# A hybrid decoder trunk on one core: filter sums on ScalarE and GpSimd, and memory preparation in split passes

## The chip, the cores and the metric

The kernel runs on one core of a Trainium2 chip. TensorE (PE in the profile) multiplies matrices; its weight loads are listed as PEld. VectorE (DVE), ScalarE (ACT) and GpSimd (POOL) do the elementwise work; SyncE (SP) issues the DMAs. The metric is the time of one execution on the device, in microseconds. Lower is better.

## The reference, cut to what matters

Two layers over 1024 tokens of width 1024, everything in float32. The change lies in the first layer's convolution and in what runs beside it.

```python
def conformer_conv(h, w_pw1, b_pw1, w_dw, b_dw, ln_g, ln_b, w_pw2, b_pw2):
    u = h @ w_pw1 + b_pw1
    a, gate = jnp.split(u, 2, axis=-1)
    u = a * jax.nn.sigmoid(gate)
    u = lax.conv_general_dilated(u, w_dw[:, None, :], window_strides=(1,),
        padding=[(CONV_WIDTH - 1, 0)], feature_group_count=D_MODEL, ...) + b_dw   # 31 taps per channel
    u = jax.nn.silu(layernorm(u, ln_g, ln_b))
    return u @ w_pw2 + b_pw2

def memory_cross_attention(h, mem_n, w_q, w_k, w_v, w_o):    # mem_n: 256 tokens, 4 heads
    s = q k^T / sqrt(256), with q = h @ w_q, k = mem_n @ w_k;  p = softmax(s)
    return (p @ (mem_n @ w_v)) @ w_o
...
x = x + conformer_conv(rmsnorm(x), ...)      # layer 0 (layer 1: attention instead)
x = x + memory_cross_attention(rmsnorm(x), rmsnorm(mem), ...)
x = x + (relu(h @ w1) ** 2) @ w2
```

## The kernel before, in words

Activations lie with the 1024 features in eight chunks of 128 partitions and the tokens along the free axis, in two halves of 512 (`HALVES`). A product that must keep float32 precision is made in split passes: an operand is split into a high part, which is a copy rounded to float32r (`act.copy`), and a low part, the difference (`low`, line 148, on VectorE). `passes` (line 262) turns a pair of split operands into three matrix instructions: low times high, high times low, high times high. An operand given as a single tile is multiplied as plain float32, in one `pe.matmul` call.

`conv_layer` (line 293) is the first layer's convolution. For each chunk `m` of channels, `gated_unit` (line 362) makes the two pointwise products on TensorE, a sigmoid on ScalarE and the gated product `u` on VectorE (line 370). `u` is kept with even and odd tokens apart, behind 15 zero columns each. `convolve` (line 386) then applies the 31 taps on VectorE. It uses a shared sum: `both` (lines 396 to 402) is a filter over the odd tokens with the sums of neighbouring taps, 16 instructions; the even outputs add 16 taps over the difference `d0`, and the odd outputs 15 taps over `d1` (line 408). The results go to `X`, and a running sum `acc` (line 354) feeds the layer norm. `layer_norm` (line 306) follows, half by half, and `linear` with `pw2` and `add_x` (line 324) ends the layer.

Beside this runs `memory_matrices` (line 433), once per layer of the whole model: per head it multiplies the memory by `wk` and `wv` (line 458), and these by `wq` and `wo` (lines 479 and 493), and stores the two combined matrices `mqk` and `mvo` in DRAM for `mem_attention`. It is a generator: each `yield` ends one step, 16 steps per layer and 32 in all. `conv_layer` takes one step at a time with `next(prep)`: two ahead of loading X, two in the normalization, two for each chunk, and the rest after the layer norm. These products are all of plain float32. Their weights come through `get` (line 438), 512 KB at a time into three buffers `praw`.

The order on each engine is made at compile time by a list scheduler: among the instructions that are ready by its own estimate, the one that was written first goes first, and `high_priority` moves one ahead. On the chip each engine works through its own list in that order and waits by semaphores. So a preparation step fills TensorE wherever gates and pw2 are not ready. Tiles named `t` in the pool `nrm` share four buffers, used by the normalizations, the squares and, with the change, the terms of the shared sum. GpSimd works in this stage only for small powers (line 207) and the zero columns (line 301).

The first MLP (lines 600 and on), which the prediction uses for comparison, has differences of 128x512 on VectorE (line 148) beside additions of 128x512 on GpSimd (lines 647, 865, 951), and additions from PSUM into SBUF on VectorE (line 967).

Of the kernel before, what the change touches and what calls it, by code (L numbers as in the profile page):

```python
# [12 lines left out]
F32 = mybir.dt.float32  # L13
# [73 lines left out]
def trunk(ctx, tc, a, out):  # L87
# [98 lines left out]
    def add_squares(acc, ch):  # L186

        sq = nrm.tile([P, HALF], F32, name="sq", tag="t", bufs=4)
# [104 lines left out]
    def conv_layer(pm, prep):  # L293
        with tc.tile_pool(name="conv", bufs=2) as cp:
# [3 lines left out]
            def padded():  # L298

                u = cp.tile([P, 2, (PAD + S) // 2], F32, name="u")  # L300
                pool.memset(u[:, :, : PAD // 2], 0.0)
                return u
# [27 lines left out]

            hs = operands()
            ahead = gate_weights(0)
            u = padded()
            for sl in HALVES:
                normalize(hs, "mix0", sl)
                next(prep)
                gated_unit(pm, cp, 0, ahead, hs, u[:, :, PAD // 2 :], sl)
            acc = [cp.tile([P, HALF], F32, name=f"acc{s}", bufs=1) for s in range(2)]
            for m in range(NCH):
                if m:  # L340
                    u = padded()
# [44 lines left out]
    def convolve(cp, m, u, sums):  # L386


        n, k = S // 2, TAPS // 2
        even, odd = u[:, 0, :], u[:, 1, :]  # L390
        d0 = cp.tile([P, n + k], F32, name="d0")
        d1 = cp.tile([P, n + k - 1], F32, name="d1")
        dve.tensor_tensor(d0, even[:, : n + k], odd[:, : n + k], op=ALU.subtract)
        dve.tensor_tensor(d1, even[:, 1 : n + k], odd[:, : n + k - 1], op=ALU.subtract)
        both = cp.tile([P, n], F32, name="both")
        dve.tensor_scalar(
            both, odd[:, :n], sums[:, 0:1], col("dw_b", m), op0=ALU.mult, op1=ALU.add
        )
        for j in range(1, k + 1):
            dve.scalar_tensor_tensor(  # L400
                both, odd[:, j : j + n], sums[:, j : j + 1], both, op0=ALU.mult, op1=ALU.add
            )
        out = [X[:, m, sl] for sl in HALVES]
        for s, d, taps in ((0, d0, k + 1), (1, d1, k)):
            y = both
            for j in range(taps):
                w = col("dw_w", m * TAPS + 2 * j + s)
                dve.scalar_tensor_tensor(  # L408
                    out[s], d[:, j : j + n], w, y, op0=ALU.mult, op1=ALU.add
                )  # L410
                y = out[s]
# [21 lines left out]
    def memory_matrices(pp, pq, layer):  # L433
# [4 lines left out]
        def get(src):  # L438
            raw = pp.tile([P, NCH, P], F32, name="praw", bufs=3)
# [1006 lines left out]
```

## Time and profile before

| | |
|---|---|
| time, median of 3 runs | 2823.84 us (2814.29 to 2826.63) |
| the profiled execution | 2825.31 us, of which the span is 2823.3 us |
| granted TensorE clock, mean | 0.991 |
| busy: PE, DVE, ACT, POOL | 2740.8, 2030.9, 1278.3, 703.1 us |
| first gated chunk complete | 76.7 us |
| first filter tap, last filter tap | 92.0, 387.7 us |
| pw2 ends | 527 us |

How to read it: the span runs from the first to the last instruction of the program in one profiled execution. A group row gives line, engine, operation, output and inputs with their shapes, count, busy time in us, mean length of one in ns, and the idle time of the engine just before, with what ended it. The length of one is longer than the pace at which such instructions follow one another, since the next starts before the last one has written everything. Ends of matrix instructions are modelled.

### The profile page before, as it was taken

Reading aid. Unit: us, or ns where it says so; the run is one execution under the profiler, and the core shown is the slowest. Engines: PE = TensorE matmul, PEld = TensorE weight load, DVE = VectorE, ACT = ScalarE, POOL = GpSimd, SP = SyncE. Lnnn points to the kernel's source line nnn. Section 1 sums busy time; section 2 is a strip of 40 time slices with the busy share of each in tenths; the row PEclk is TensorE's granted clock in tenths of the full one; section 3 lists DMA queues with packets and bytes.
Section 4 is the critical chain, followed back from the end, with each engine's and each line's share of the span. In section 5 each row is a group of like instructions: output and inputs, shape, how many; then the busy total and the mean of one; then the engine's idle time right before and its main releaser. Section 6 shows DMA issues by size and latency. Waiting matters only on the chain.

```text
span 2823.3 us, 36214 instructions
## 1 busy us (share of the span) xinstructions
PE 2740.8 (97%) x12968; PEld 2261.3 (80%) x12968; DVE 2030.9 (72%) x3358; ACT 1278.3 (45%) x2293; POOL 703.1 (25%) x473
## 2 busy tenths in 40 slices
PE   8999999999999999999899999989999999989998
PEld 6777777888888877888688888878888788878886
DVE  5999984555776576777788888875546855577776
ACT  5212143433555553333466666673423655543332
POOL 0000000000065625774000000000000365525773
PEclk9999999999999999999899999999999999999999
DMA  6334364322165585652222221243213455655651
GB/s 219 120 119 135 114 206 124 101 90 70 65 230 177 178 309 187 227 199 89 69 68 70 57 65 55 69 136 98 94 64 105 149 176 190 218 208 197 227 201 61
DMA packets 165428, 390.68 MB, mean 138 GB/s; under 512 B 17264, under 2 KB 46192, under 8 KB 164992
## 3 DMA queue, kind: packets, MB, share of 16 engines
q1 hardware_dynamic: 165248, 388.37, 40.9%
q8 instruction: 102, 1.67, 0.2%
q14 instruction: 78, 0.64, 0.1%
HBM read 270.79 MB, written 113.31 MB: 136 GB/s over the span
## 4 chain that ended last, share of the span: by engine, by line
PE 74%; DVE 12%; ACT 5%; DMA 5%; issue 3%; POOL 1%; SPq 0%; DVEq 0%; POOLq 0%; ACTq 0%
PE mm L1070 34%; PE mm L269 29%; PE mm L1255 5%; DVE w L148 2%; DVE op L148 2%; DVE x L408 1%; PE mm L1341 1%; DVE x L1310 1%; DMA ua<-x 1%; ACT x L1315 1%; PE mm L1353 1%; PE mm L1354 1%; DVE both L400 1%; DVE wl L148 1%; ACT pth L151 1%
## 5 line engine op out<-in xcount | busy, mean ns | idle before, releaser
L1070 PE MATMUL mm<-op,w 128*128 128x512 f32 x5424 | 1242.4, 391 | 24.5 <-ACT m L955 8.7
L1070 PEld LDWEIGHTS mm<-op,w 128*128 128x128 f32 x5424 | 1020.5, 189 | 243.2 <-ACT m L955 9.6
L269 PE MATMUL mm<-op,wh 128*128 128x512 f32 x1056 | 330.5, 394 | 4.2 <-DVE op L148 4.2
L148 DVE TENSOR_TENSOR w<-r,w 128x512 fp32r<-128x512 f32 x264 | 262.6, 998 | 30.5 <-ACT w L653 30.5
L653 ACT CAST w<-r 128x512 fp32r<-128x512 f32 x264 | 163.3, 622 | 262.0 <-PE mm L1070 233.2
L269 PEld LDWEIGHTS mm<-op,wh 128*128 128x128 f32 x1056 | 200.2, 190 | 48.5 <-DVE op L148 6.5
L1255 PE MATMUL mm<-op,wh 128*128 128x512 f32 x736 | 231.4, 396 | 0.0
L148 DVE TENSOR_TENSOR w<-t,w 128x512 fp32r<-128x512 f32 x180 | 178.2, 1005 | 63.2 <-ACT w L653 63.1
L269 PE MATMUL mm<-op,wl 128*128 128x512 f32 x528 | 210.5, 400 | 7.1 <-DVE wl L148 6.2
L207 POOL TENSOR_TENSOR r<-v,mhalf 128x4 f32<-128x4 f32 (+1 forms) x15 | 16.8, 1117 | 741.0 <-DVE v L205 741.0
L647 POOL TENSOR_TENSOR t<-r,t 128x512 f32<-128x512 f32 x104 | 174.9, 1681 | 91.4 <-DVE w L148 54.2
L653 ACT CAST w<-t 128x512 fp32r<-128x512 f32 x180 | 112.0, 622 | 169.8 <-PE mm L1070 140.6
L151 ACT CAST wh<-raw 128x1024 fp32r<-128x1024 f32 x96 | 100.7, 1050 | 193.8 <-PE mm L269 97.5
L865 POOL TENSOR_TENSOR x<-x,x 128x512 f32<-128x512 f32 x112 | 160.2, 1455 | 112.6 <-ACT x L878 101.6
L967 DVE TENSOR_TENSOR x<-mm,x 128x512 f32<-128x512 f32 x160 | 109.5, 684 | 91.1 <-PE mm L1070 73.7
L1255 PEld LDWEIGHTS mm<-op,wh 128*128 128x128 f32 x736 | 139.2, 189 | 26.7
L269 PE MATMUL mm<-op,xsh 128*128 128x512 f32 x512 | 158.0, 393 | 0.0
L1255 PE MATMUL mm<-op,wl 128*128 128x512 f32 x368 | 155.0, 421 | 1.9 <-ACT q L1275 1.9
L151 ACT CAST pth<-mm 128x512 fp32r<-128x512 f32 (+1 forms) x224 | 105.9, 495 | 108.5 <-PE mm L556 80.8
L408 DVE SCALAR_TENSOR_TENSOR x<-d,par,x 128x512 f32<-128x512 f32 x232 | 154.5, 746 | 0.0
L647 POOL TENSOR_TENSOR t<-r,r 128x512 f32<-128x512 f32 x52 | 80.2, 1542 | 295.1 <-DMA r<-in_ff_w 191.0
L1315 ACT ACTIVATE x<-x,nb 128x128 f32<-128x128 f32 (+7 forms) x128 | 99.5, 778 | 109.3 <-DVE nb L1313 100.0
(188 smaller groups left out, 4689.6 us busy)
## 6 DMA issues: line engine op xcount, KB each, us to landing
r<-in_ff_w SPq DMA_DIRECT2D x128, 512.0 KB, 4.0
op<-ua SPq DMA_DIRECT2D x80, 512.0 KB, 6.8
us<-x SPq DMA_DIRECT2D x128, 256.0 KB, 2.9
op<-us SPq DMA_DIRECT2D x64, 512.0 KB, 5.6
raw<-mvo SPq DMA_DIRECT2D x32, 512.0 KB, 3.4
ua<-ul SPq DMA_DIRECT2D x64, 256.0 KB, 2.2
ua<-uh SPq DMA_DIRECT2D x60, 256.0 KB, 2.3
raw<-in_pw SPq DMA_DIRECT2D x24, 512.0 KB, 4.7
```

The costliest lines, as they stand in the source:

```text
L148: dve.tensor_tensor(lo, src, hi.bitcast(F32), op=ALU.subtract)
L151: act.copy(hi, src)
L269: pe.matmul(out_ps, x, y, start=i == 0, stop=i == len(terms) - 1)
L400: dve.scalar_tensor_tensor(both, odd[:, j : j + n], sums[:, j : j + 1], both, op0=ALU.mult, op1=ALU.add)
L408: dve.scalar_tensor_tensor(out[s], d[:, j : j + n], w, y, op0=ALU.mult, op1=ALU.add)
L647: (dve if g in (2, 3, UP, UP + 1) else pool).tensor_tensor(t, raws[g, x], raws[g, y], op=ALU.subtract)
L653: act.copy(highs[n][0], raws[steps[n][:2]])
L865: eng.tensor_tensor(u[g, x], y1, y2, op=op_)
L967: dve.tensor_tensor(v, sums[key], v, op=ALU.add)
L1070: pe.matmul(sums[key], y, z, start=first and i == 0, stop=n == last_of[key] and i == len(terms) - 1, skip_group_check=True,)
L1255: pe.matmul(t, x, y, start=n == 0, stop=n == len(terms) - 1)
L1315: act.activation(x[:, :n], x[:, :n], AF.Exp, bias=nb, accum_out=rs)
```

## The change

The shared sum moves out of `convolve` into `shared_sum`: each of the 16 terms is a multiplication on ScalarE, and 15 additions on GpSimd gather them in `both`. It is written one chunk ahead of the filters, and the gates two chunks ahead, with three fixed tiles `planes` for `u`. In `convolve` the taps add up in one PSUM bank, `acc = bank(pc)`, which both the even and the odd chain use; only the last tap of each writes to `X`. The preparation's pool has three PSUM banks instead of four.

`memory_matrices` splits its operands. The memory is loaded in four pieces and split by ScalarE (high, with the gain) and VectorE (low). `get` loads each weight in two halves; ScalarE makes the high part and GpSimd the low part. The products of keys and values are split as they are read from PSUM. All its products are now made in three passes. Of its 32 steps, two more than before are taken ahead of the layer norm.

```diff
-            for m in range(NCH):
-                if m:
-                    u = padded()
-                    for sl in HALVES:
-                        gated_unit(pm, cp, m, ahead, hs, u[:, :, PAD // 2 :], sl)
-                if m + 1 < NCH:
-                    ahead = gate_weights(m + 1)
+            shared = shared_sum(cp, 0, planes[0], pairs[:, 0])
+            for m in range(-1, NCH):
+                if m + 2 < NCH:
+                    ahead = gate_weights(m + 2)
                 for _ in range(2):
                     next(prep, None)
-                convolve(cp, m, u, pairs[:, m])
+                if m + 2 < NCH:
+                    for sl in HALVES:
+                        gate(m + 2, ahead, sl)
+                if m < 0:
+                    continue
+                now = shared
+                if m + 1 < NCH:
+                    shared = shared_sum(cp, m + 1, planes[(m + 1) % 3], pairs[:, m + 1])
+                convolve(cp, pc, m, planes[m % 3], now)
...
+    def shared_sum(cp, m, u, sums):
+        n, k = S // 2, TAPS // 2
+        odd = u[:, 1, :]
+        both = cp.tile([P, n], F32, name="both")
+        act.activation(both, odd[:, :n], AF.Identity, scale=sums[:, 0:1], bias=col("dw_b", m))
+        for j in range(1, k + 1):
+            t = nrm.tile([P, HALF], F32, name="tap", tag="t", bufs=4)
+            act.activation(t, odd[:, j : j + n], AF.Copy, scale=sums[:, j : j + 1])
+            pool.tensor_tensor(both, both, t, op=ALU.add)
+        return both
...
-        out = [X[:, m, sl] for sl in HALVES]
+        acc = bank(pc)
         for s, d, taps in ((0, d0, k + 1), (1, d1, k)):
             y = both
             for j in range(taps):
+                o = X[:, m, HALVES[s]] if j == taps - 1 else acc
                 w = col("dw_w", m * TAPS + 2 * j + s)
-                dve.scalar_tensor_tensor(
-                    out[s], d[:, j : j + n], w, y, op0=ALU.mult, op1=ALU.add
-                )
-                y = out[s]
+                dve.scalar_tensor_tensor(o, d[:, j : j + n], w, y, op0=ALU.mult, op1=ALU.add)
+                y = acc
...
         def get(src):
-            raw = pp.tile([P, NCH, P], F32, name="praw", bufs=3)
-            nc.sync.dma_start(raw, src)
-            return raw
+            halves = []
+            for i in range(2):
+                raw = half(src[:, 4 * i : 4 * i + 4, :])      # one load of 256 KB, three buffers
+                hi, lo = (pp.tile([P, NCH // 2, P], F32R, name=f"p{x}", bufs=3) for x in "hl")
+                act.copy(hi, raw)
+                pool.tensor_tensor(lo, raw, hi.bitcast(F32), op=ALU.subtract)
+                halves.append((hi, lo))
+            return halves
...
-                    product(t[:, c, :], [((x[:, k, :],), (mem[:, k, :],)) for k in range(NCH)])
+                    product(t[:, c, :], [
+                        ([y[:, k % 4, :] for y in x[k // 4]], (memh[:, k, :], meml[:, k, :])) for k in range(NCH)
+                    ])
...
-    with prep_pools(4) as pools, banks(2) as pm:
-        conv_layer(pm, chain(*(memory_matrices(*pools, l) for l in range(2))))
+    with prep_pools(3) as pools, banks(2) as pm, banks(1) as pc:
+        conv_layer(pm, pc, chain(*(memory_matrices(*pools, l) for l in range(2))))
```

More of the change, by code (lines that the diff above doesn't have):

```diff
@@ L436, in memory_matrices, with half @@
         ad, vd = mats[layer]
+        def half(src):
+            raw = pp.tile([P, NCH // 2, P], F32, name="praw", bufs=3)
+            nc.sync.dma_start(raw.rearrange("p k n -> p (k n)"), src.rearrange("p k n -> p (k n)"))
+            return raw
         def get(src):
[L439 to L444 removed]
+            halves = []
[6 more added lines that the diff above has]
+            return halves
+        memh, meml = (pp.tile([P, NCH, MEM], F32R, name=f"mem{x}", bufs=1) for x in "hl")
+        sums = None
+        for c in range(NCH):
+            if c % 2 == 0:
+                two = half(a["memT"][:, c : c + 2, :]).rearrange("p (c k) n -> p c (k n)", c=2)
+            ch, g = two[:, c % 2, :], col(f"src{layer}", c)
+            if layer == 0:
+                sums = add_squares(sums, ch)
+            act.activation(memh[:, c, :], ch, AF.Copy, scale=g)
+            dve.scalar_tensor_tensor(
+                meml[:, c, :], ch, g, memh[:, c, :].bitcast(F32), op0=ALU.mult, op1=ALU.subtract
+            )
         if layer == 0:
[L446 removed]
+            with tc.high_priority(offset=SMALL_FIRST):
+                r = rms_of_sums(sums, RMS_EPS)
             rt = const.tile([P, MEM // P], F32, name="mem_r")
@@ L449, in memory_matrices @@
             mem_r.extend((rt, rs))
-        for c in range(NCH):
-            act.activation(mem[:, c, :], mem[:, c, :], AF.Copy, scale=col(f"src{layer}", c))
         for h in range(MEM_HEADS):
```

46 lines of the change are left out of this document (19 added, 27 removed).

## The prediction

> **What bounds the kernel now.** I read the busy table of the page first, then the stage of the change cut into stretches, then its instructions by group, and its sequence in order of time.
>
> ```profile
> PE 2740.8 (97%) x12968; PEld 2261.3 (80%) x12968; DVE 2030.9 (72%) x3358; ACT 1278.3 (45%) x2293; POOL 703.1 (25%) x473
> ```
>
> The whole kernel looks bound by TensorE, but a change in one stage is worth what that stage's last wait is worth. The table by stretches (columns: stretch in us, its length, busy us and instruction count of PE, PEld, DVE, ACT, POOL, granted clock, DMA share, GB/s) has these cuts: up to the first gated chunk; up to the first filter tap; the filters; the layer norm; the second pointwise product (pw2).
>
> ```profile
> core 0 of [0], span 2823.3 us
> core 0: us, PE busy (x) PEld busy (x) DVE busy (x) ACT busy (x) POOL busy (x), PEclk, DMA share, GB/s
> 0.00:77.00 77.00, 63.62 (x254) 49.19 (x255) 40.51 (x69) 38.68 (x69) 3.54 (x11) 0.96 0.61 207
> 77.00:92.00 15.00, 15.00 (x70) 13.07 (x70) 14.47 (x21) 0.59 (x1) 0.01 (x1) 1.00 0.49 159
> 92.00:389.00 297.00, 292.35 (x1230) 230.48 (x1229) 292.10 (x421) 63.10 (x105) 0.74 (x6) 1.00 0.42 135
> 389.00:442.00 53.00, 52.22 (x242) 39.95 (x243) 39.83 (x67) 38.20 (x68) 2.01 (x2) 1.00 0.52 163
> 442.00:527.00 85.00, 85.00 (x370) 68.96 (x368) 32.12 (x40) 22.27 (x32) 0.00 (x0) 1.00 0.35 104
> ```
>
> From 92 to 389 VectorE (292.1 of 297) and TensorE (292.4) are both full, and GpSimd does nothing (0.74). VectorE is full of work that nothing can replace; TensorE is full because the preparation of the memory matrices runs wherever it fits. The stage ends by a VectorE path (last filter tap, layer norm, pw2) and a TensorE path (gates, preparation, pw2) that are almost equally long. So each must get shorter for the time to fall. Behind 527 nothing is edited.
>
> **TensorE.** The preparation's products are plain float32; each shows as two instructions. Groups, then sequences in time (start, length, count), then two pieces of the chain of waits that hold split-pass products of 512 and of 256 columns:
>
> ```profile
> L269 PE MATMUL mm<-mem,praw 128*128 128x256 f32 x512 | 116.7, 386 | 9.1 <-ACT mem L451 8.7 <-DMA praw<-in_mem_wk 0.5
> ...
> L269 PE MATMUL mm<-kt,praw 128*128 128x256 f32 x256 | 61.2, 385 | 6.0 <-ACT o L483 4.5 <-DMA praw<-in_mem_wq 1.4
> L269 PE MATMUL mm<-praw,vt 128*128 128x512 f32 x128 | 59.1, 594 | 0.0
> ```
> ```profile
> 57.98 7.03 PE L269 MATMUL mm<-praw,vt 128*128 128x512 f32 x16
> ...
> 75.74 13.97 PE L269 MATMUL mm<-mem,praw 128*128 128x256 f32 x64
> ```
> ```profile
> 557.15 5.49 PE mm L269 x24
> ...
> 574.92 5.75 PE mm L269 x48
> ```
>
> Before: 768 instructions of 256 columns at 13.97/64 = 0.218 us and 128 of 512 at about 0.43 (7.03 less the last one's tail of 0.16, by 16): 167 + 55 = 222 us. After, 384 and 64 products of three passes each: 384 x 3 x 5.75/48 = 138 and 64 x 3 x 5.49/24 = 44, together 182. TensorE loses **40 us**. That is the most this change can bring, and only if no other engine is late.
>
> **VectorE.** The filters by group in 77 to 389, then their order in time:
>
> ```profile
> L408 DVE SCALAR_TENSOR_TENSOR x<-d,par,x 128x512 f32<-128x512 f32 x232 | 154.5, 746 | 0.0
> L400 DVE SCALAR_TENSOR_TENSOR both<-u,sums,both 128x512 f32<-128x512 f32 x120 | 90.2, 752 | 4.1
> ...
> L354 DVE TENSOR_TENSOR acc<-acc,x 128x512 f32<-128x512 f32 x14 | 9.0, 686 | 0.0
> ...
> L396 DVE TENSOR_SCALAR both<-u,sums,par 128x512 f32<-128x512 f32 x8 | 4.3, 543 | 0.0
> L466 DVE TENSOR_TENSOR kt<-mm,mem_rs 128x512 f32<-128x512 f32 x6 | 4.1, 685 | 1.0 <-PE mm L269 1.0
> ```
> ```profile
> 75.94 0.75 DVE L370 SCALAR_TENSOR_TENSOR u<-mm,par,sg 128x512 f32<-128x512 f32 x1 [2.56 <-PE mm L269]
> ...
> 91.97 1.42 DVE L408 SCALAR_TENSOR_TENSOR x<-d,par,both 128x512 f32<-128x512 f32 x2
> ```
> ```profile
> 311.35 2.34 DVE L148 TENSOR_TENSOR wl<-raw,wh 128x1024 fp32r<-128x1024 f32 x2
> ...
> 315.42 8.63 DVE L400 SCALAR_TENSOR_TENSOR both<-u,sums,both 128x512 f32<-128x512 f32 x11
> ...
> 329.10 15.99 DVE L408 SCALAR_TENSOR_TENSOR x<-d,par,x 128x512 f32<-128x512 f32 x24
> ```
>
> The two rows L400 and L408 at 315 and 329 show a pace. A shared-sum step waits for the one before it (each adds into the same tile): 8.63/11 = 0.785 us. The taps belong to two independent chains, the even and the odd outputs, that alternate: 15.99/24 = 0.666. The new code gives both chains one PSUM tile, so the second chain cannot begin before the first has read its last value. The taps become one dependent chain.
>
> From first to last tap, against the 297 us of before:
> - Shared sums of chunks 1 to 7 leave: 105 x 0.785 + 7 x 0.57 = -86.
> - 248 taps go from 0.666 to the dependent pace: 248 x 0.12 = +30. No row here has VectorE writing PSUM. Bounds: 0.666 (no cost) and 0.785 plus as much again as the dependence costs, 0.90 (+58). I take 0.785, the nearest row, since an addition that reads PSUM takes no longer than one from SBUF (L466 685 against L354 686).
> - One gate and two weight differences move ahead of the first tap: -2 x 0.66 - 2 x 1.13 = -4.
> - New differences for the preparation: about 11 of 128x512 at 0.6, and 8 half-wide ones for the second layer's memory at about 0.43: +10.
> - Waits for GpSimd. The following rows are of the first MLP (groups and stretch 715 to 1340), where GpSimd works beside VectorE, and of whole lines (min/median/max in ns).
>
> ```profile
> 715.00:1340.00 625.00, 615.83 (x2723) 508.28 (x2724) 448.88 (x540) 301.91 (x493) 336.10 (x214) 1.00 0.53 185
> ```
> ```profile
> L148 DVE TENSOR_TENSOR w<-r,w 128x512 fp32r<-128x512 f32 x132 | 133.3, 1013 | 15.3 <-ACT w L653 15.3
> L148 DVE TENSOR_TENSOR w<-t,w 128x512 fp32r<-128x512 f32 x90 | 89.1, 1006 | 29.9 <-ACT w L653 29.9
> L148 DVE TENSOR_TENSOR op<-op 128x1024 fp32r<-128x1024 f32 x40 | 59.7, 1493 | 0.0
> ```
> ```profile
> L148 DVE TENSOR_TENSOR w<-r,w x264: 675/689/1820, 714.9 to 2787.6; 128x512 fp32r<-128x512 f32 x132
> ```
> ```profile
> L967 DVE TENSOR_TENSOR x<-mm,x x160: 674/682/693, 1060.0 to 2807.5; 128x512 f32<-128x512 f32 x160
> ```
> ```profile
> L647 POOL TENSOR_TENSOR t<-r,t x104: 1286/1622/2302, 790.9 to 2768.8; 128x512 f32<-128x512 f32 x104
> ```
> ```profile
> L647 POOL TENSOR_TENSOR t<-r,t 128x512 f32<-128x512 f32 x52 | 87.9, 1691 | 41.1 <-DVE w L148 21.2 <-DMA ua<-ul 17.9
> ```
>
> An operation with two SBUF operands takes 0.69 us alone and 1.01 on average here: +0.33 with GpSimd busy 336/625 = 54%. One operand in PSUM, and nothing is lost (L967 never over 693). So the PSUM taps are safe, and what waits is: the two differences of a chunk, the first tap of each chain, the two sums for the norm, the weight differences and those of kt: 8 x 4 + 14 + 12 + 5 = 63. GpSimd does 105 sum steps and some 68 low parts in that stretch, 173 x 1.29 = 223 us of 280, 80%. So 63 x 0.33 x 80/54 = +31. Bounds: 0, and a whole GpSimd operation each, 63 x 1.29 = +81; the scaled row stands nearest to the case.
>
> Sum: -86 + 30 - 4 + 10 + 31 = **-19**.
>
> First tap: the chunk's u is there at 76.7. Then 15 additions on GpSimd, at least 1.286 each (19.3), one ScalarE step of 0.6 and about four low parts between them (5.2): 101.8 against 91.97, **+10**. The start up to 76.7 I cost at nothing: TensorE has some 6 us less in it, while the first products now also wait for a copy on ScalarE and a subtraction on GpSimd, and X stands behind more and smaller loads in SP's queue (bounds -4 and +8; the cover is VectorE, busy 40.5 of 77).
>
> Layer norm: its first half can begin one chain (15 x 0.785 = 12 us) before the last tap, so that these gaps get covered, 6 us:
>
> ```profile
> 390.12 0.16 DVE L310 TENSOR_SCALAR nm<-mm 128x4 f32<-128x4 f32 x1 [1.15 <-PE mm L158]
> 391.55 4.88 DVE L314 TENSOR_TENSOR x<-x,mm 128x512 f32<-128x512 f32 x8 [1.27 <-PE mm L167]
> ...
> 403.09 0.16 DVE L205 TENSOR_SCALAR v<-mm 128x4 f32<-128x4 f32 x1 [1.29 <-PE mm L158]
> 405.59 0.69 DVE L317 TENSOR_TENSOR x<-x,mm 128x512 f32<-128x512 f32 x1 [2.34 <-PE mm L167]
> ```
>
> Against it stand 30 operations with two SBUF operands, while GpSimd still makes the last low parts in less than half of the norm: 30 x 0.49 x 0.4 = +6. Together 0.
>
> The VectorE path is 19 - 10 = **9 us shorter**. TensorE then has some 30 us with nothing to do ahead of pw2, and its 40 us are not the limit.
>
> The other edits at nothing: 128 ScalarE copies and 128 tap products of 0.52 to 0.62 us are 140 us on an engine that is busy 63 of 297; smaller loads carry the same bytes; the third buffer for u takes the wait off the gates; three PSUM banks instead of four cost only if the copies out of them are late. GpSimd's whole work is 248 x 1.29 = 320 us plus waits, done by about 395, ahead of pw2 at about 420. If it isn't, TensorE waits for low parts, and the norm pays the port longer.
>
> **Where the Trainium skill says otherwise.** The Trainium skill, Perfetto Trace Analysis, section Optimizing Scalar/DVE Operations, gives about 60 ns of data access per VectorE instruction on SBUF and 125 on PSUM. By that the 248 taps would cost about 16 us more (an estimate from that page), and the sum would be +7 instead of -9. The rows above that read PSUM show no such difference; for writing PSUM nothing here shows it.
>
> **The rivals.**
> A, the forecast: VectorE sets the end, 9 us shorter. The sum is made against the profiled execution (2825.3, its span 2823.3 and 2.0 around it), which lies 1.5 above the median 2823.84; from the median: **2815 us**. Its own range is 2802 to 2828.
> B, TensorE sets the end: if the taps keep 0.666 (-30) or the port costs nothing (-31), the VectorE path is 40 us shorter, and all of TensorE's 40 count: 2784; with half of either 2800. For it: PSUM reads are no slower, and independent operations slip between dependent taps. Against it: one tile for both chains.
> C, slower: GpSimd sets the pace of the sums. By the seventh sum it has 120 sum steps and 64 low parts; at 1.29 that is 237 us, ending at 314, no limit. At 1.64, about the mean of its rows in the MLP (1691 above), it is 302, ending at 379, and the last filter (31 x 0.785 and two sums, 26) at 405 against 389: 2840. It decides from about 1.6 us per operation; at 1.69 it gives 2848. For it: the same contention, seen from the other side, and ScalarE must hand each term over. Against it: in the MLP operations with two SBUF operands fill (133.3 + 89.1 + 59.7)/625 = 45% of VectorE's time, here about 16%.
> D, a dependent tap through PSUM lies half-way to its upper bound, 0.785 + 0.06 = 0.845: 248 x 0.06 = +15, giving 2830, still within 0.5%. Nothing here shows a VectorE write to PSUM, which leaves it open; the PSUM reads speak against it.
>
> **How the numbers follow.** I give A 0.42, B 0.25, C 0.19, D 0.14. A measurement of this kernel tells about 0.5%, 14 us, from no change: faster is below 2810, slower above 2838. A holds a third of its share below 2810; C lies above 2838 nearly whole; D a fifth. Faster 0.25 + 0.14 = 0.39; slower 0.19 + 0.03 = 0.22; same 0.39. The range from 2784 (B whole) to 2846 (C nearly whole) leaves out 2 in 10.
>
> **What would show it.** Taps at a start-to-start pace of 0.78 (B: 0.67; D: 0.84). First tap near 102, last near 380. GpSimd near 320 us more in the first 400, mean operation 1.3 to 1.4 (C: over 1.6). Operations of L148 with two SBUF operands near 1.2 us in the filters, taps unaffected. TensorE idle for some 30 us before pw2, which ends near 518 instead of 527. The prediction is wrong if the start shifts by more than 8 us, or if TensorE stands waiting for low parts within the filters.

## The result: 4.8% slower, and the profile after

The changed kernel takes 2955.4 us (median of 4 runs, 2954.5 to 2959.4) against 2822.5 for the kernel before on the same chip: a ratio of 1.048, 95% interval 1.045 to 1.050. That is outside the predicted range (2784 to 2846) and above the slower rival's 2848. The busy table of the page, and the stage cut at the changed kernel's own events (first gated chunk, first tap, last tap, end of the norm, end of pw2; columns as in the prediction):

```profile
PE 2757.8 (93%) x13416; PEld 2300.1 (78%) x13416; DVE 2009.9 (68%) x3262; ACT 1436.4 (49%) x2557; POOL 1040.0 (35%) x716
```
```profile
0.00:87.00 87.00, 59.27 (x314) 50.75 (x315) 50.23 (x79) 48.81 (x89) 30.65 (x31) 0.94 0.56 184
87.00:109.00 22.00, 11.31 (x63) 9.58 (x62) 3.43 (x3) 13.28 (x21) 19.37 (x15) 0.86 0.08 25
109.00:472.00 363.00, 299.93 (x1493) 251.94 (x1493) 271.74 (x338) 180.92 (x302) 254.53 (x187) 0.90 0.35 109
472.00:524.00 52.00, 30.77 (x161) 26.80 (x161) 37.25 (x57) 33.43 (x55) 12.10 (x9) 0.70 0.17 50
524.00:648.00 124.00, 117.63 (x577) 95.81 (x575) 35.19 (x44) 43.38 (x72) 26.66 (x21) 1.00 0.46 138
```

Set against the five stretches of before: the first tap comes 17 us later (109 for 92), the filters take 66 us more (363 for 297), the norm 1 us less, and the way from there to the end of pw2 39 us more (124 for 85). That is 121 of the 129 us by which the span grew. Up to the end of the norm no engine is full any more: in the filters TensorE is busy 300 of 363, VectorE 272, GpSimd 255, ScalarE 181. Nobody is short of time; all of them wait.

One row of each kernel, up to the same point of the program (the first score product of the memory attention, at 524.9 us before and 646.6 after), shows what the waiting cost. First the kernel before, then the changed one:

```profile
0.00:524.90 524.90, 506.09 (x2152) 400.09 (x2153) 417.04 (x612) 161.41 (x271) 6.30 (x19) 0.99 0.45 143
```
```profile
0.00:646.60 646.60, 518.06 (x2600) 434.50 (x2601) 396.45 (x516) 319.05 (x535) 343.30 (x262) 0.90 0.38 117
```

TensorE stood idle for 18.8 us before (524.9 - 506.1) and for 128.5 after: +110. Its busy time should have fallen by the 40 us of passes saved, but it rose by 12; the granted clock fell from 0.99 to 0.90. So some 52 us more went into products at a slower clock (an estimate from these two rows and the 40 us of the prediction), and +110 +12 make up the 122 us.

Who waited for whom in the changed kernel, from the list of waits up to 600 us (us in total, times, longest):

```profile
POOL pl L461 <- ACT ph L460: 106.5, 47, 15.5
DVE mm L421 <- POOL both L405: 83.2, 8, 21.3
...
PE mm L269 <- POOL pl L461: 62.5, 37, 12.1
POOL both L405 <- ACT tap L404: 60.3, 5, 15.0
...
PE mm L269 <- ACT kth L151: 16.9, 1, 16.9
```

VectorE waits for GpSimd's sums, GpSimd waits for ScalarE's terms and high parts, TensorE waits for GpSimd's low parts, and ScalarE in turn waits for TensorE (30.6 us in eight waits for the gates' first products alone). One turn of this, chunk 2 to chunk 3, in order of time (start, length, engine; in brackets the idle time before it and what ended it): VectorE, then GpSimd, then TensorE.

```profile
209.93 1.77 DVE L421 SCALAR_TENSOR_TENSOR mm<-d,par,both 128x512 f32<-128x512 f32 x1 [6.63 <-POOL both L405]
211.74 2.34 DVE L421 SCALAR_TENSOR_TENSOR mm<-d,par,mm 128x512 f32<-128x512 f32 x3
213.98 0.75 DVE L377 SCALAR_TENSOR_TENSOR u<-mm,par,sg 128x512 f32<-128x512 f32 x1
...
224.22 0.75 DVE L377 SCALAR_TENSOR_TENSOR u<-mm,par,sg 128x512 f32<-128x512 f32 x1
...
255.72 1.76 DVE L421 SCALAR_TENSOR_TENSOR mm<-d,par,both 128x512 f32<-128x512 f32 x1 [13.40 <-POOL both L405]
```
```profile
227.23 1.93 POOL L405 TENSOR_TENSOR both<-both,tap 128x512 f32<-128x512 f32 x1 [13.18 <-ACT tap L404]
229.12 2.98 POOL L461 TENSOR_TENSOR pl<-praw,ph 128x512 fp32r<-128x512 f32 x2
232.06 6.75 POOL L405 TENSOR_TENSOR both<-both,tap 128x512 f32<-128x512 f32 x5
238.76 4.70 POOL L461 TENSOR_TENSOR pl<-praw,ph 128x512 fp32r<-128x512 f32 x3
243.42 12.27 POOL L405 TENSOR_TENSOR both<-both,tap 128x512 f32<-128x512 f32 x9
```
```profile
214.78 0.50 PE L269 MATMUL mm<-op,wl 128*128 128x512 f32 x1 [3.22 <-DVE u L377]
```

Filters 2 start the moment sum 2 is complete (209.93). The gated signal of chunk 3 stands on VectorE's list behind their first four taps (213.98); TensorE, whose two gate banks are full, waits for it and makes the second half only then; that half's `u` comes at 224.22, sum 3 can start, and at 255.72 filters 3 start the moment it is complete. The sum is written one chunk ahead, but it is not ahead on the chip: it is a link of a closed ring, 45.8 us a turn. The kernel before needed 39 (first taps of chunks 0 and 7 at 92.0 and 366.5 us, seven turns apart). GpSimd meanwhile spends 13 us with nothing to do, and its five low parts stand between the additions that the ring waits for.

### The profile page after: what moved, and what is told of

Read it like the earlier page. It is cut to its first block, busy times and chain, and to the rows that moved or that the text cites. A ratio compares the mean times of both kernels' runs of the same rounds, so it can differ in the third digit from the quotient of the medians.

```text
span 2952.3 us, 37897 instructions
## 1 busy us (share of the span) xinstructions
PE 2757.8 (93%) x13416; PEld 2300.1 (78%) x13416; DVE 2009.9 (68%) x3262; ACT 1436.4 (49%) x2557; POOL 1040.0 (35%) x716
## 4 chain that ended last, share of the span: by engine, by line
PE 63%; DVE 8%; ACT 5%; issue 5%; DMA 4%; POOL 2%; SPq 0%; POOLq 0%; DVEq 0%; ACTq 0%
PE mm L1106 34%; PE mm L269 18%; PE mm L1291 5%; DVE op L148 1%; DVE w L148 1%; POOL pl L461 1%; PE mm L1377 1%; DVE x L1346 1%; ACT x L1351 1%; PE mm L1389 1%; PE mm L1390 1%; ACT pth L151 1%; PE mm L1341 1%; PE mm L1342 1%; DMA r<-in_ff_w 1%
## 5 line engine op out<-in xcount | busy, mean ns | idle before, releaser
L269 PE MATMUL mm<-op,wl 128*128 128x512 f32 x528 | 210.8, 400 | 15.8 <-DVE u L377 5.3
L461 POOL TENSOR_TENSOR pl<-praw,ph 128x512 fp32r<-128x512 f32 x128 | 176.6, 1396 | 110.7 <-ACT ph L460 106.5
L405 POOL TENSOR_TENSOR both<-both,tap 128x512 f32<-128x512 f32 x120 | 161.5, 1346 | 68.3 <-ACT tap L404 60.3
L421 DVE SCALAR_TENSOR_TENSOR mm<-d,par,mm 128x512 f32<-128x512 f32 x216 | 162.9, 754 | 5.7
```

What stands on the lines that cost most here:

```text
L269: pe.matmul(out_ps, x, y, start=i == 0, stop=i == len(terms) - 1)
L405: pool.tensor_tensor(both, both, t, op=ALU.add)
L421: dve.scalar_tensor_tensor(o, d[:, j : j + n], w, y, op0=ALU.mult, op1=ALU.add)
L461: pool.tensor_tensor(lo, raw, hi.bitcast(F32), op=ALU.subtract)
```

## The experiments

Ratios are to the kernel before on the same chip in the same series, with 95% intervals. A difference between two runs of different series is one of medians on different chips, and good to some 5 us. A turn is the time from the first tap of one chunk to that of the next, the mean of seven. First come the two halves alone, then the ring, the low parts and the end of the memory products.

**The halves alone.** The convolution half: the memory products stay plain float32, `memory_matrices` as before.

> The convolution's half of the change alone (shared sum on ScalarE and GpSimd, gates two chunks ahead, taps in PSUM), with the memory preparation as it was before, in plain float32 and without low parts. Theory Q (queues tied in a ring: TensorE's gate stands behind preparation products, these behind low parts on GpSimd, these behind the steps of a sum or behind copies whose buffers TensorE still holds): without low parts the ring is open, TensorE waits for GpSimd no longer, period per chunk 36 to 39 us, time 2805 to 2840. Rival S (the shared sum is itself the late link: gated product, 26 us of sum, filter): the period stays near 45, 2900 or more. Rival L (GpSimd has too much to do): its work halves, period near 38.

Measured: 2913.0 us, 1.032 (1.029 to 1.035), as rival S has it. A turn takes 46.1 us (first taps from 95.2 to 418.0).

The memory half: convolution as before, `memory_matrices` as changed.

> The preparation's half of the change alone (split passes, low parts on GpSimd), with the convolution as it was before, all on VectorE. Theory Q: no sum steps stand between low parts, but copies and low parts still run only three half weights ahead: some waits of TensorE for low parts stay (10 to 30 us), filters as before at 39 us a chunk: 2815 to 2850. Rival S: nothing of the loss is left, 2800 to 2825. Rival L: the same as S, since GpSimd has 165 us in all.

Measured: 3019.7 us, 1.070 (1.068 to 1.072). The half alone loses more than the whole. TensorE waits 102.9 us for low parts in it (62.5 in the whole), and TensorE's memory products end at 640 us, 80 us after the layer norm. GpSimd's 128 low parts take 257.4 us in it, against 176.6 in the whole change. They read SBUF beside taps that have both operands in SBUF, and one low part took 13.6 us while VectorE ran 24 such taps in a row. VectorE, GpSimd and TensorE:

```profile
321.47 15.98 DVE L408 SCALAR_TENSOR_TENSOR x<-d,par,x 128x512 f32<-128x512 f32 x24
```
```profile
324.97 13.60 POOL L450 TENSOR_TENSOR pl<-praw,ph 128x512 fp32r<-128x512 f32 x1 [4.68 <-ACT ph L449]
```
```profile
338.63 0.79 PE L269 MATMUL mm<-pl,vth 128*128 128x512 f32 x1 [12.87 <-POOL pl L450]
```

In the whole change, where the taps add up in PSUM, the longest low part took 1.8 us. So part of this half's loss is VectorE and GpSimd getting in each other's way, and the convolution half takes that part away. My first theory, that the loss comes from the two halves sharing ScalarE and GpSimd, fell with these two: each half loses by itself, and the halves don't add up.

**Moving work between the queues.** Low parts of the memory weights on VectorE:

```diff
-                pool.tensor_tensor(lo, raw, hi.bitcast(F32), op=ALU.subtract)
+                low(lo, raw, hi)
```

> The changed kernel with the preparation's low parts on VectorE instead of GpSimd (128 differences of 128x512, 0.69 us each); the sums stay on GpSimd. Theory Q: the ring goes through VectorE now, behind single filter taps instead of whole 1.3 us steps, so it is shorter but not open: 2850 to 2920, period 38 to 42. Rival S: the sum alone needs 15 x 1.29 = 20 us instead of 26 to 28: 6 us less per chunk, about 2905. Rival L: GpSimd's load falls from 30 to 20 us per chunk and is no limit any more: VectorE's 31 + 5 us set the period, 2830 or less.

Measured: 2931.9 us, 1.039 (1.037 to 1.041). It is 24 us better than the change, no more: TensorE then waits 39.6 us for low parts made by VectorE, which stand behind taps. It is above all three forecasts.

Gates written ahead of the two memory steps instead of behind them:

```diff
+                if m + 2 < NCH: (both gate halves)
                 for _ in range(2):
                     next(prep, None)
-                if m + 2 < NCH: (both gate halves)
```

> The changed kernel with one order exchanged: in each chunk the gate two chunks ahead is written before the two preparation steps, not after them, so TensorE takes it first. Theory Q: the gate no longer stands behind products that wait for low parts, the sum of the next chunk can start while this one's filter runs: period from 45 down to 36 to 40, 2860 to 2910. Rival S: the gate is earlier here too, so the sum is ready ahead: also better; the two differ by TensorE's waits for low parts, which by S would stay near 62 us and by Q fall within the filters. Rival L: GpSimd has the same load, period unchanged near 45, 2940 to 2960.

Measured: 2977.3 us, 1.055 (1.053 to 1.057): worse. The gates do run ahead (u of chunk 2 is complete at 165.8), but its sum starts only at 207.2, behind eleven low parts on GpSimd's list that wait for high parts from ScalarE, up to 18 us at a time. No theory had this.

**Is it ScalarE's queue?** The convolution half, with GpSimd adding the shifted planes directly, so that ScalarE makes no terms (the kernel leaves the scaling out):

```diff
-            act.activation(t, odd[:, j : j + n], AF.Copy, scale=sums[:, j : j + 1])
-            pool.tensor_tensor(both, both, t, op=ALU.add)
+            pool.tensor_tensor(both, both, odd[:, j : j + n], op=ALU.add)
```

> The convolution half alone, with GpSimd adding the shifted planes directly: the 15 products by ScalarE of each shared sum are left out (the sum is unscaled), the 15 additions on GpSimd stay. With the products it took 2913 us. Theory Q2 (ScalarE's queue: its 15 products of a sum go at GpSimd's pace through 4 buffers, and the sigmoid of the next gate and the evictions of the memory products stand behind them, so that TensorE runs out of banks; it waited some 38 us for the gate's second operation and 40 us for evictions, beside clock lost after each wait): 2825 to 2855. Rival L (the 21 us of a sum on GpSimd stand in series between a gate and its filters, whoever feeds them): 2890 to 2915, and filters still start 44 to 48 us apart.

Measured: 2916.0 us, 1.034 (1.031 to 1.036), as with the terms. ScalarE's terms are not the cause in this half; the rival with the sum in series fits. The same edit in the whole change:

> The changed kernel with GpSimd adding the shifted planes directly: ScalarE's 15 products of each shared sum are left out (the sum is unscaled), the additions and the low parts on GpSimd stay. Changed kernel: 2955 us. Theory S (ScalarE's queue is the main block, for the high parts too): 2840 to 2890. Theory Q2 in the form that GpSimd's queue is the main one: 2920 to 2950.

Measured: 2984.4 us, 1.057 (1.055 to 1.059), 29 us worse than the change; TensorE's waits for low parts rise from 62.5 to 90.6 us. Why they rise was not followed further. The memory half with GpSimd's zeroing of the planes moved out of the loop:

```diff
-                u = cp.tile([P, 2, (PAD + S) // 2], F32, name="u")
-                pool.memset(u[:, :, : PAD // 2], 0.0)
+                u = planes[m % 2]            # two fixed planes, zeroed once
```

> The memory half alone, with the convolution's planes zeroed once at the start and not once per chunk, so that GpSimd has no zeroing between the low parts. The half alone took 3020 us. Theory Q2 (in-order queues: a zeroing waited for VectorE's old plane, 69 us in all, with all low parts of the weights behind it): 2920 to 2970. Rival W (GpSimd's own time for the low parts, or ScalarE's copies, sets the pace): 3005 to 3025.

Measured: 3017.6 us, 1.069 (1.067 to 1.071): a miss. The zeroing's 69 us of waiting went, and GpSimd's wait for high parts grew from 190.0 to 263.9 us in its place. A long wait in the list is not a cost by itself.

**The ring.** The convolution half again, with one order added: VectorE issues a chunk's filters only behind both halves of the next chunk's `u`.

```diff
-                convolve(cp, pc, m, planes[m % 3], now)
+                with tc.issue_after(done[min(m + 1, NCH - 1)].ins):   # the last u of gate m+1
+                    convolve(cp, pc, m, planes[m % 3], now)
```

> The convolution half alone, with one order added: VectorE issues the filters of a chunk only behind both halves of the next chunk's gated signal. Without it the half took 2913 us. Theory R (a ring through VectorE's queue: the next gate's signal stands 12 to 16 taps deep in filters that wait for their own sum, so that sum m+1 starts only after filters m have; 15 us of taps + 10 of the gate's second half + 21 of the sum = 47 a chunk): the ring is cut, filters start about 40 us apart, as TensorE allows, and the time is 2825 to 2860. Rival L (the sum stands in series whatever the order): 2900 to 2920. Rival Q2 (ScalarE's queue blocks TensorE): 2890 or more, with the same waits of TensorE for evictions.

Measured: 2852.5 us, 1.012 (1.011 to 1.014): 60 of the half's 92 us came back, and a turn takes 36.6 us (first taps from 110.5 to 366.8). The order has a price of its own: the first tap comes 15 us later than without it, since the filters of chunk 0 now wait for the `u` of chunk 1. The half without the order, VectorE and GpSimd in order of time:

```profile
234.34 0.76 DVE L421 SCALAR_TENSOR_TENSOR mm<-d,par,both 128x512 f32<-128x512 f32 x1 [16.07 <-POOL both L405]
...
243.72 0.75 DVE L377 SCALAR_TENSOR_TENSOR u<-mm,par,sg 128x512 f32<-128x512 f32 x1
...
254.41 0.74 DVE L377 SCALAR_TENSOR_TENSOR u<-mm,par,sg 128x512 f32<-128x512 f32 x1
...
278.35 0.76 DVE L421 SCALAR_TENSOR_TENSOR mm<-d,par,both 128x512 f32<-128x512 f32 x1 [12.20 <-POOL both L405]
```
```profile
256.70 21.61 POOL L405 TENSOR_TENSOR both<-both,tap 128x512 f32<-128x512 f32 x15 [22.39 <-ACT tap L404]
```

9.4 us of taps, 10.7 to the second half of `u`, 2.3 to the sum, 21.6 for the sum: 44 us a turn. With the order, the same two engines:

```profile
223.92 1.78 DVE L424 SCALAR_TENSOR_TENSOR mm<-d,par,both 128x512 f32<-128x512 f32 x1
...
256.47 0.75 DVE L380 SCALAR_TENSOR_TENSOR u<-mm,par,sg 128x512 f32<-128x512 f32 x1 [1.81 <-PE mm L269]
...
259.50 0.75 DVE L424 SCALAR_TENSOR_TENSOR mm<-d,par,both 128x512 f32<-128x512 f32 x1
```
```profile
223.33 21.91 POOL L408 TENSOR_TENSOR both<-both,tap 128x512 f32<-128x512 f32 x15 [16.60 <-ACT tap L407]
```

Now the next chunk's sum (223.33) runs beside the filters (223.92), VectorE no longer waits for GpSimd, and the chunks follow at 34 to 39 us. TensorE in the stretch from 92 to 400, without and with the order:

```profile
92.00:400.00 308.00, 254.52 (x1011) 196.10 (x1010) 213.90 (x274) 116.13 (x183) 128.43 (x95) 0.92 0.27 90
```
```profile
92.00:400.00 308.00, 293.47 (x1234) 229.18 (x1234) 250.87 (x323) 138.05 (x223) 146.73 (x107) 1.00 0.40 130
```

The order in the whole change:

> The whole changed kernel with the same order added (filters behind the next chunk's gated signal on VectorE). Without it: 2955 us. Theory R with the low parts as a second cause (GpSimd needs 22 us of low parts and 20 of a sum per chunk, and TensorE waits for the low parts): the ring is cut but the low parts still hold TensorE: 2900 to 2940. If the ring were all: 2850 or less. If the low parts were all: 2945 to 2965.

Measured: 2935.7 us, 1.043 (1.041 to 1.044): 20 us. A turn falls to 41.3 us, but the first tap comes at 136.8 instead of 109.2, which takes much of that back. The 22 us of low parts per chunk in this expectation was a miscount; 81 of the 128 fall into the filters' stretch, ten a chunk, 14 us. TensorE's wait for them stays at 62.5 us. With the low parts on VectorE and the order:

> The changed kernel with the low parts of the memory weights on VectorE and the same order added. With the low parts on VectorE alone it took 2932 us. Theory R with the low parts as a second cause: both causes are eased, 2840 to 2890. If the low parts on VectorE, behind filters, hold TensorE just as much: 2920 or more.

Measured: 2943.1 us, 1.045 (1.043 to 1.046): no gain over the low parts on VectorE alone (2931.9); the two remedies don't add.

**What is left of the convolution half.** The ring cut, and the two chains alternating into their output planes again, with four banks for the memory products:

```diff
-        acc = bank(pc)
...
-                o = X[:, m, HALVES[s]] if j == taps - 1 else acc
+                o = acc = X[:, m, HALVES[s]]
...
-    with prep_pools(3) as pools, banks(2) as pm, banks(1) as pc:
+    with prep_pools(4) as pools, banks(2) as pm:
```

> The convolution half alone with the order that cuts the ring (2852 us), its two tap chains alternating into their output planes as before the change, and so four PSUM banks for the memory products again. If the remaining 34 us are the bank (TensorE waits 29 + 14 us for evictions) and the slower taps: 2820 to 2836. If they are the start (first filter 18 us later, since a sum takes 20 us on GpSimd and waits for the next gate): 2843 to 2855.

Measured: 2921.6 us, 1.035 (1.033 to 1.038): 69 us worse, which no theory had. The groups of the tap and of the addition from 92 to 400, with the chains in SBUF, then in PSUM (the half with the order):

```profile
L423 DVE SCALAR_TENSOR_TENSOR x<-d,par,x 128x512 f32<-128x512 f32 x174 | 197.5, 1208 | 0.0
L408 POOL TENSOR_TENSOR both<-both,tap 128x512 f32<-128x512 f32 x93 | 150.0, 1613 | 138.5 <-ACT tap L407 131.7
```
```profile
L424 DVE SCALAR_TENSOR_TENSOR mm<-d,par,mm 128x512 f32<-128x512 f32 x216 | 163.0, 754 | 6.6
L408 POOL TENSOR_TENSOR both<-both,tap 128x512 f32<-128x512 f32 x107 | 146.8, 1372 | 117.1 <-ACT tap L407 109.3
```

A tap with both operands in SBUF takes 1208 ns beside GpSimd, against 746 in the kernel before, where GpSimd was idle; GpSimd's addition grows to 1613. With the accumulator in PSUM a tap takes 754 and an addition 1372. So the shared bank, which the prediction charged 30 us for, is worth more than it costs. All remedies together, with those chains and the low parts split between VectorE and GpSimd:

> The whole change with the remedies together: filters behind the next chunk's gated signal, chains alternating into the output planes, four banks for the memory products, and the low part of every first half weight on VectorE, of every second on GpSimd. Ring cut and each pair of low parts ready in half the time: 2840 to 2890. If the low parts hold TensorE as much as on one engine: 2915 or more. Faster than the kernel before (under 2805) only if TensorE's 40 us of saved passes come through whole.

Measured: 2997.0 us, 1.062 (1.059 to 1.064). The taps take 1310 ns there and the additions 1596, the same price, so this run says nothing of the split low parts.

**The low parts.** One constant tile in place of the low parts, in the whole change. The kernel leaves GpSimd's 128 subtractions out; TensorE's three passes stay:

```diff
-                pool.tensor_tensor(lo, raw, hi.bitcast(F32), op=ALU.subtract)
-                halves.append((hi, lo))
+                halves.append((hi, lows))            # one tile, written once
```

> The changed kernel with one constant tile in place of the low parts of the memory weights: GpSimd's 128 low parts are left out, TensorE's three passes, ScalarE's high parts and the shared sums stay. Changed kernel: 2955 us. Theory Q2 (TensorE's 62 us of waits for low parts, and the clock lost after them, come from the low parts standing in GpSimd's queue behind the sums): 2850 to 2890. Rival S (ScalarE's queue, blocked by the products of the sums, delays high parts just the same): 2920 to 2950.

Measured: 2893.5 us, 1.024 (1.022 to 1.027): 62 us, as expected; a turn takes 41.2 us (first taps from 101.0 to 389.5). In the memory half alone:

> The memory half alone with one constant tile in place of the low parts of its weights: GpSimd's 128 low parts are left out, TensorE's three passes and ScalarE's high parts stay. With the low parts it took 3020 us. If the hand-over of low parts through GpSimd is what costs (TensorE waited 103 us for them): 2800 to 2850. If high parts, copied by ScalarE behind evictions and sigmoids into buffers for one and a half weights, hold TensorE as well: 2880 to 2940.

Measured: 2901.7 us, 1.030 (1.028 to 1.031): 118 us of that half's 198, with the contention shown above among them. The other 80 are not in the filters: these keep nearly their old pace, the last tap at 398.5 us for 387.8. TensorE, in order of time, after its last product at 350.5:

```profile
399.75 1.87 PE L158 MATMUL mm<-mean_col,acc 128*128 128x1 f32 x8 [49.26 <-DVE acc L354]
...
440.32 1.01 PE L269 MATMUL mm<-kth,fix 128*128 128x256 f32 x3 [16.86 <-ACT kth L151]
```

The norm's mean product stands on TensorE's list ahead of the memory products that are left. It waits 49 us for the last filter, and they wait behind it. Then comes another such place, which the changed kernel has too: the high part of `kt` (`kth`), 16.9 us: `kt` stands behind the norm's work on VectorE, and its copy behind the norm's squares on ScalarE. In the kernel before, the mean waited 0.57 us, with memory products on either side of it.

**The memory products that are left**, written ahead of the norm, first in the memory half with the constant tile:

```diff
+            for _ in prep:
+                pass
             for s in range(2):
                 layer_norm(s, acc[s])
-            for _ in prep:
-                pass
```

> The memory half alone with a constant tile for the low parts (2902 us), and the memory products that remain after the last chunk written ahead of the layer norm instead of behind it. Theory H (TensorE's queue: the layer norm's mean products wait 49 us for the last filter, with all remaining memory products behind them; those then run beside and after the layer norm and hold back the pointwise products): the wait goes, 2835 to 2870. Rival (the high parts on ScalarE set the pace of the memory products at the end, wherever they are queued): 2890 to 2910.

Measured: 2859.8 us, 1.013 (1.010 to 1.016): 42 us, as that theory has it. The half still takes 40 us more than the kernel before; these were not traced.

**Together.** The whole change with the order and the constant tile:

> The whole changed kernel with the order that cuts the ring and a constant tile in place of the low parts of the memory weights. Order alone: 2936 us; constant tile alone: 2894 us. If ring and low parts are separate causes and add up: 2860 to 2880. If the ring is only hidden behind the low parts (it gives the 60 us of the convolution half once they are gone): 2825 to 2850. If another cause holds TensorE: 2885 or more.

Measured: 2880.3 us, 1.020 (1.017 to 1.023): the two causes add, nearly (20 and 62 alone, 75 together), and a turn takes 35.5 us (first taps from 125.1 to 373.4). With the third edit too:

> The whole change with the order that cuts the ring, a constant tile for the low parts, and the remaining memory products written ahead of the layer norm. Without the last: 2880 us. If those products, behind the layer norm's mean, are the third cause, as in the memory half alone (2902 to 2860): 2830 to 2855. If they are hidden here: 2872 to 2888.

Measured: 2865.6 us, 1.016 (1.014 to 1.018): 15 us, between the two forecasts. And with the low parts kept:

> The whole change, low parts kept on GpSimd, with both orders: filters behind the next chunk's gated signal, remaining memory products ahead of the layer norm. With the first order alone: 2936 us. If the third cause is worth 25 to 45 us here too: 2890 to 2912. If the low parts set the pace of those products wherever they stand: 2925 to 2945.

Measured: 2925.8 us, 1.037 (1.035 to 1.040): 10 us, as expected if the low parts set the pace of those products wherever they stand; TensorE still waits 66.6 us for them. What still separates the version with all three waits removed from the kernel before shows in its stretches (to the first tap; filters; norm; to the first score product):

```profile
0.00:123.60 123.60, 95.83 (x522) 84.01 (x523) 53.40 (x88) 71.16 (x128) 23.74 (x27) 0.94 0.46 155
123.60:406.00 282.40, 263.36 (x1453) 226.02 (x1452) 251.75 (x332) 176.97 (x299) 141.13 (x105) 0.96 0.44 143
406.00:476.30 70.30, 48.74 (x270) 41.98 (x269) 36.39 (x60) 50.29 (x88) 2.02 (x2) 0.78 0.42 131
476.30:558.20 81.90, 81.90 (x363) 67.81 (x362) 30.90 (x38) 18.82 (x26) 0.00 (x0) 1.00 0.26 81
```
```profile
461.19 1.86 PE L158 MATMUL mm<-mean_col,acc 128*128 128x1 f32 x8 [15.04 <-DVE acc L183]
```

The filters are 13 us shorter than before (282.4 for 295.8): there the saved work does show. But the first tap is 32 us later, since it now waits for a sum on GpSimd and for the next gate, and the norm is 16 us longer (70.3 for 54.2): TensorE has used up its memory products ahead of the norm and waits 15 us within it, with nothing to fill the time, for the sum of squares (the last row). 31.6 - 13.4 + 16.1 - 1.0 = 33 us, of 45 in the time. No version beat the kernel before. The rest, and the 7 us that the changed kernel loses behind the first score product, were not traced.

## Why the prediction was wrong

Right were most of its prices. The taps run at 9.45/12 = 0.787 us (taken: 0.785):

```profile
229.64 9.45 DVE L421 SCALAR_TENSOR_TENSOR mm<-d,par,mm 128x512 f32<-128x512 f32 x12
```

A chain through PSUM runs as fast as the dependent chain through SBUF of before, which decides against rival D (0.845). The Trainium skill, Perfetto Trace Analysis, section Optimizing Scalar/DVE Operations, has a VectorE instruction spend about twice as long on data access in PSUM as in SBUF; no such difference shows here, and the measurement decides. GpSimd's additions take 1346 and its low parts 1396 ns (given: 1.3 to 1.4), so rival C did not decide by its rule. Groups of the changed kernel, from 87 to 472 us:

```profile
L421 DVE SCALAR_TENSOR_TENSOR mm<-d,par,mm 128x512 f32<-128x512 f32 x216 | 162.9, 754 | 5.7
L405 POOL TENSOR_TENSOR both<-both,tap 128x512 f32<-128x512 f32 x120 | 161.5, 1346 | 68.3 <-ACT tap L404 60.3
...
L421 DVE SCALAR_TENSOR_TENSOR mm<-d,par,both 128x512 f32<-128x512 f32 x16 | 20.4, 1275 | 83.3 <-POOL both L405 83.2
...
L414 DVE TENSOR_TENSOR d<-u 128x526 f32<-128x526 f32 x8 | 13.4, 1671 | 0.0
```

Operations with two SBUF operands take longer beside GpSimd, as charged: the 16 first taps 1275 ns for 750, the 13 sums for the norm 1335 for 686, the differences 1671 and 1027 (eight each) for 702. That is some 27 us of the 31. The 15 weight differences, which were charged too, paid nothing (1220 for 1217). VectorE's work did get shorter, by 24 us up to the norm's end (363 for 387, summed over the stretches).

The step that failed is the shared sum's: "Shared sums of chunks 1 to 7 leave", -86 us, with GpSimd's 248 operations under "The other edits at nothing" because their total, 320 us, fits into 395. The sum's latency was charged once, for the first chunk (+10), and taken as hidden for the other seven because the sum is written one chunk ahead. I did not ask where the `u` that feeds it stands on VectorE's list. It stands in filters that wait for their own sum, so the latency came back on every chunk. In the convolution half cutting that ring alone took a turn from 46.1 to 36.6 us and gave 60 us. In the whole change the low parts share the 66 us that the filters lost: a turn takes 46.3 us, 41.3 with the order alone, 41.2 with the constant tile alone, 35.5 with both (39.2 before), so the two cost some 5 us a turn each. Nor did the third buffer for `u` take "the wait off the gates": TensorE waits for VectorE to read their banks, 3.2 us at 214.78, and VectorE does so within those filters. Rival C asked about GpSimd's throughput over the stage, and that was not the limit: GpSimd is idle for 108 of the 363 us of the filters.

The second failure is the line beside it, "If it isn't, TensorE waits for low parts". The cover named was a total again, "done by about 395"; the last low part ended at 569 us. Leaving the low parts out gave 62 us in the whole; that takes TensorE's waits away and also the low parts between the ring's additions, and no run parts the two. Why they come late is an estimate that no run tested, for instance with more buffers: the low parts can be at most three half weights ahead, so they are made while TensorE multiplies; GpSimd needs 2.8 us per weight (2 x 1.396) and TensorE about 2.9 (24 passes at 0.12), which leaves no slack for an addition in between. The prediction had named the sign, TensorE waiting for low parts within the filters, but gave the case no time.

The third is "TensorE then has some 30 us with nothing to do ahead of pw2", at no cost. In the memory half with the constant tile TensorE's idle time came ahead of the norm's mean product, with memory products queued behind it, so what was saved before the mean was paid after it: 42 us. In the changed kernel the mean waits for nothing; the like place there is the 16.9 us wait for `kth` within the norm, and writing those products ahead of the norm gave 10 to 15 us. The start came 10 us late (86.8 for 76.7; with the constant tile 78.6), just outside the bounds of -4 and +8.

Fourth, idle time was counted once where TensorE pays twice, by the clock (below): some 52 us of the 122.

## What to carry to other kernels

Where two engines are both full, as TensorE and VectorE were here (292 of 297 us each), they stand in step because each one's list fits the other's, and work moved to two idle engines adds hand-overs that must fit as well: follow one item round the loop through every engine's list (gate, sum, filter, next gate) and add up the latencies before adding up totals. A buffer depth says how far ahead a producer can be; if it is less than the consumer's burst, the producer's rate counts inside the burst, not over the stage. Code written ahead is ahead on the chip only if the instruction that feeds it stands ahead on its own engine's list.

## What the runs showed of the hardware

TensorE's clock halved after a long wait. In the changed kernel, three-pass products of 256 columns follow each other at 0.12 us while TensorE is kept busy, and at 0.21 after the 9.6 us wait for a low part:

```profile
222.09 0.28 PE L269 MATMUL mm<-ktl,ph 128*128 128x256 f32 x1
222.21 0.28 PE L269 MATMUL mm<-kth,ph 128*128 128x256 f32 x1
...
434.70 0.58 PE L269 MATMUL mm<-memh,pl 128*128 128x256 f32 x1 [9.59 <-POOL pl L461]
435.07 0.42 PE L269 MATMUL mm<-meml,ph 128*128 128x256 f32 x1
435.29 0.41 PE L269 MATMUL mm<-memh,ph 128*128 128x256 f32 x1
```
```profile
434.70:440.60 5.90, 5.90 (x27) 5.90 (x28) 5.65 (x8) 0.95 (x2) 4.15 (x3) 0.50 0.43 133
```

The slow pace lasted until 440.6, 5.9 us, at a granted clock of 0.50 (1.00 in the 4.4 us behind it). After a wait of 1.1 us, at 226.2, the pace stayed at 0.12. The Trainium skill, TensorE: Matmul & The Clock Gate, section Part 1: The HAM clock gate (the "warmup" mystery), describes this: half rate after an idle window of about 3.4 us, full rate after a busy one. The trace agrees with the halving. The Trainium skill's figure there of under 1% of a span is for the ramp as a kernel starts; here the waits come in every chunk, and the estimate of 52 us is 1.8%.

VectorE and GpSimd held each other up where both read SBUF. Beside GpSimd's additions a tap with two SBUF operands took 1208 instead of 746 ns, about the 0.49 us more that the prediction took for one operation (0.33 x 80/54). Which side waits differs: in the memory half alone the taps kept 754 ns, and a low part on GpSimd took up to 16.8 us (1.26 at the least). The Trainium skill, SBUF — State Buffer, section Who interferes with whom, says that a VectorE instruction with two SBUF inputs contends with a GpSimd instruction that reads SBUF, and that one with at most one does not; taps with one operand in PSUM, at 754 ns beside GpSimd, agree.
